# Attention scores from fp32 q and k, loaded once per pair of heads, with 64-row products and two units a round

## The chip, the cores and the metric

The kernel runs on one core of a Trainium2 chip. The metric is device time in microseconds; three executions of the kernel before took 2005.05 us in the median (2004.14 to 2009.55). The engines have a queue each and work through it in order: TensorE (PE, with its weight loads, PEld), VectorE (DVE), ScalarE (ACT), GpSimd (POOL) and SyncE (SP), which here only issues DMA transfers.

## The reference

One layer of a hybrid decoder, for a prompt group (1 sequence of 1024 tokens) and a sample group (8 sequences, one new token each, with 2048 cached keys and values). Only the attention half of the mixer is touched:

```
h = modulate(x, sh1, sc1);  q, k, v, z, xbc, dt_raw = split(h @ w_in)
q = rope(q) * 64**-0.5;  k = rope(k)                       # 16 heads of 64
parts = [dilated attention(q, k, v) for (window, dilation) in ((128, 1), (512, 4), (2048, 16))]
attn = parts merged by weights proportional to their softmax denominators
mix = concat(rms_norm(attn) * g_attn, gated SSD output) @ w_out;  x = x + g1 * mix;  then an MLP and a final norm
```

A prompt query reads itself and the keys at distances d, 2d, ..., window. A sample query reads the same distances in its cache.

## The kernel before, in words

The order of the work is written out by hand: each engine's instructions stand in the order in which the program emits them. A main stream is a generator whose yields state a cost, and `Side` streams are emitted beside it in proportion to these costs. Three stages matter here.

*The q and k projection* (`proj_qk`, 570 to 763 us of the trace). Each of 8 weight blocks goes through four ranges of 256 tokens and two feature halves f; a half is 8 k-tiles of three float32r products (`mm3`, L62 to L64), 48 products for both halves (509 products ran from 600 to 660 us of the trace). DVE multiplies each half with cos and sin (L679), `rotated` mixes them (L627, L628) into the tile `ab`, ACT casts that to a float32r high half `hl` (L634), DVE subtracts for the low half (L635), and the store to `q_d` or `k_d` (L637) follows. What is put off goes into the list `self.later`, one entry of which is emitted at each half of a feature half; its third entry, `turn`, transposes the rotated k on TensorE (L648, L652) for the cache output. Beside the projection run the end of the SSD and `sample_ssd` (ACT L1015, POOL L1016, L1026 and L1027, DVE L1023), then the attention's first loads (`prep(0)`, the mask, `load_v(0)`).

*The attention of the prompt* (`attention`, 763 to 1026 us). A head pair j has 16 units (j, kind, i): eight of kind B (dilations 4 and 16, among the tokens of one residue mod 4) and then eight of kind A (dilation 1). A unit covers 128 queries of both heads and 128 or 256 keys. Keys lie in DRAM residue by residue. `prep` loads per head three float32r tiles of 128 rows: q high over q low, k high over low, and k low over high, 24 transfers for a pair. `scores(n)` makes, for each of the two heads, two products over 128 rows (L1276, L1277); for kind B the stationary q is a slice with a step of four columns. DVE adds the mask, takes the negated maximum and writes P (L1279). `exps(n - 1)` (L1288) follows one unit later, `transposes(n - 3)` (L1297, copied out of PSUM by ACT or DVE, L1299) and `pv(n - 6)` (L1314), the product with v on a 64-column tile for each head. One round of the loop is one unit, and on TensorE it is: scores, transposes, pv. `merge(j)` joins kinds A and B: the statistics of B go through DRAM to reach token order (`st_d`, loaded back into `J`, L1333), some ten small operations on DVE follow (L1338 to L1350), and four groups of four transposes (L1361).

*The sample's scores* (`decode_scores`), a side stream from the 12th unit on. For 24 pieces of the cached keys POOL multiplies 128x1024 values with q (L1089) and halves them twice by additions (L1093), DVE sums the rest (L1095), and the next piece is fetched by a DMA (L1071). Three buffers `dkv` hold the pieces; piece n is summed while piece n + 1 is worked on.

PSUM has eight banks: three for `s`, three for `pt`, two for `o`.

## Time and profile before

| | |
|---|---|
| time of three executions | 2005.05 us median, 2004.14 to 2009.55 |
| profiled execution, span from first to last instruction | 2009.0 us; the page shows no time of it beside the span; the slowest of the three, 2009.55, is the nearest |
| q and k projection | about 570 to 763 us |
| attention of the prompt, with the sample's scores | 763 to 1026 us |
| mean granted TensorE clock over the span | 0.983 of full speed |

The two stages are 456 us of the span; the input projection, the SSD, the output projection and the MLP, which are not changed, make up the rest. The page gives the busy time of each engine; a view by stretch gives it for a part of the span, with the clock that TensorE was granted (1.00 is 2.4 GHz, half of it 1.2 GHz) and the share of the 16 DMA engines. A busy TensorE is not TensorE at its peak: how fast it gets on is read from the distance between the starts of its instructions. An idle time stands with what ended it; "issue" is time in which the engine waited for nothing that the profile shows.

### The profile page before, as it was taken

The numbers are of one execution on the slowest core, as the hardware profiler recorded it, in microseconds if no ns is written. First come the engines' busy times: TensorE is split into PE (matmuls) and PEld (weight loads), VectorE is DVE, ScalarE is ACT, GpSimd is POOL, SyncE is SP. The second block draws the span as 40 slices with busy tenths as digits, with TensorE's granted clock in tenths as the row PEclk, the third lists the DMA queues.
The fourth block names the chain that finished last, engine by engine and source line by source line (L and its number), as shares of the span: only waits on it lengthen the run. The fifth ranks groups of instructions, "written<-read, shape, count | busy, mean of one in ns | idle before, by whom it ended". The sixth has DMA issues, their size and how long they took to land.

```text
span 2009.0 us, 34179 instructions
## 1 busy us (share of the span) xinstructions
PE 1918.1 (95%) x13390; PEld 1792.7 (89%) x13390; DVE 1219.6 (61%) x2966; ACT 700.8 (35%) x1681; POOL 356.8 (18%) x310
## 2 busy tenths in 40 slices
PE   5999999999999789999998999999999999999998
PEld 3689999999999787777786899999999999999997
DVE  4614675674787876767773444655555555555566
ACT  3511425344443335656652232422211122222212
POOL 0010143342320640565610012000000000000000
PEclk8999999999999888999999999999999999999999
DMA  9672222222346869999846310557765566657664
GB/s 285 251 273 82 74 66 64 86 60 77 118 144 192 256 187 222 228 211 228 203 164 219 121 43 22 210 210 251 252 230 210 210 251 250 232 210 251 250 242 169
DMA packets 200267, 366.81 MB, mean 183 GB/s; under 512 B 29728, under 2 KB 163488, under 8 KB 195713
## 3 DMA queue, kind: packets, MB, share of 16 engines
q1 hardware_dynamic: 196524, 351.27, 55.1%
q0 software_dynamic: 3376, 13.30, 2.1%
q8 instruction: 106, 1.74, 0.4%
q14 instruction: 53, 0.43, 0.1%
q10 hardware_dynamic: 208, 0.07, 0.0%
HBM read 321.64 MB, written 177.23 MB: 248 GB/s over the span
## 4 chain that ended last, share of the span: by engine, by line
PE 49%; DMA 5%; DVE 4%; POOL 1%; SPq 1%; issue 1%; ACT 1%; DVEq 0%; POOLq 0%; ACTq 0%
PE acc L62 15%; PE acc L63 14%; PE acc L64 14%; DMA dkv<-in_cache_k_win 2%; PE o L1314 1%; PE pt L1297 1%; PE s L1276 1%; DMA st_d<-st 1%; SPq L1236 1%; PE misc L1162 1%; PE s L1277 1%; PE otr L1534 1%; POOL dkv L1089 1%; DMA dkv<-in_cache_v_win 1%; POOL dkv L1093 0%
## 5 line engine op out<-in xcount | busy, mean ns | idle before, releaser
L1406 DVE SCALAR_TENSOR_TENSOR x<-acc,mod,x 128x352 f32<-128x352 f32 (+2 forms) x432 | 238.8, 561 | 149.0 <-PE acc L64 142.4
L62 PE MATMUL acc<-u,mw_hi 128*128 128x352 f32 (+3 forms) x800 | 251.7, 315 | 0.3 <-DVE gs L1410 0.3
L63 PE MATMUL acc<-u,mw_hi 128*128 128x352 f32 (+3 forms) x800 | 251.1, 314 | 0.0
L64 PE MATMUL acc<-u,mw_lo 128*128 128x352 f32 (+3 forms) x800 | 250.4, 313 | 0.0
L63 PE MATMUL acc<-h_lo,mw_hi 128*128 128x352 f32 (+1 forms) x720 | 230.3, 320 | 0.0
L62 PE MATMUL acc<-h_hi,mw_hi 128*128 128x352 f32 (+1 forms) x720 | 229.8, 319 | 0.0
L64 PE MATMUL acc<-h_hi,mw_lo 128*128 128x352 f32 (+1 forms) x720 | 229.6, 319 | 0.0
L62 PE MATMUL acc<-h_hi,cw_hi 128*128 128x352 f32 (+1 forms) x576 | 191.8, 333 | 1.1 <-ACT cw_hi L442 1.1
L63 PE MATMUL acc<-h_lo,cw_hi 128*128 128x352 f32 (+1 forms) x576 | 184.1, 320 | 0.0
L64 PE MATMUL acc<-h_hi,cw_lo 128*128 128x352 f32 (+1 forms) x576 | 183.7, 319 | 0.2 <-DVE cw_lo L443 0.2
L1723 ACT ACTIVATE ur<-acc 128x352 f32<-128x352 f32 (+1 forms) x96 | 43.8, 456 | 394.3 <-PE acc L64 394.3
L1724 DVE TENSOR_TENSOR ur<-ur 128x352 f32<-128x352 f32 (+1 forms) x96 | 49.6, 516 | 169.0 <-ACT ur L1723 169.0
L62 PE MATMUL acc<-h_hi,qw_hi 128*128 128x256 f32 (+1 forms) x512 | 152.1, 297 | 0.0
L62 PEld LDWEIGHTS acc<-u,mw_hi 128*128 128x128 f32 x800 | 150.4, 188 | 1.1 <-PE acc L64 0.5
L64 PEld LDWEIGHTS acc<-u,mw_lo 128*128 128x128 f32 x800 | 150.6, 188 | 0.0
L63 PEld LDWEIGHTS acc<-u,mw_hi 128*128 128x128 f32 x800 | 150.3, 188 | 0.0
L64 PE MATMUL acc<-h_hi,qw_lo 128*128 128x256 f32 (+1 forms) x512 | 147.0, 287 | 2.0 <-DVE qw_lo L443 2.0
L63 PE MATMUL acc<-h_lo,qw_hi 128*128 128x256 f32 (+1 forms) x512 | 147.1, 287 | 0.0
L1288 ACT ACTIVATE P<-P,st 128x256 f32<-128x256 f32 (+1 forms) x256 | 119.3, 468 | 74.1 <-DVE st L1279 73.9
L63 PEld LDWEIGHTS acc<-h_lo,mw_hi 128*128 128x128 f32 x720 | 135.4, 188 | 0.0
L62 PEld LDWEIGHTS acc<-h_hi,mw_hi 128*128 128x128 f32 x720 | 135.3, 188 | 0.0
L64 PEld LDWEIGHTS acc<-h_hi,mw_lo 128*128 128x128 f32 x720 | 135.2, 188 | 0.0
(422 smaller groups left out, 4604.6 us busy)
## 6 DMA issues: line engine op xcount, KB each, us to landing
aw<-in_w_ada SPq DMA_DIRECT2D x16, 1024.0 KB
mw_raw<-in_w_down SPq DMA_DIRECT2D x16, 1024.0 KB
out_k_win_sample<-in_cache_k_win SPq DMA_DIRECT2D x8, 2044.0 KB
out_v_win_sample<-in_cache_v_win SPq DMA_DIRECT2D x8, 2044.0 KB
mw_raw<-in_w_up SPq DMA_DIRECT2D x15, 1024.0 KB
cw_raw<-in_w_in SPq DMA_DIRECT2D x24, 512.0 KB
dkv<-in_cache_k_win SPq DMA_DIRECT2D x24, 512.0 KB
dkv<-in_cache_v_win SPq DMA_DIRECT2D x24, 512.0 KB
```

Source lines behind the costliest of these rows:

```text
L62: mm(ps, lhi, rhi, start=first, stop=False)
L63: mm(ps, lhi, rlo, start=False, stop=False)
L64: mm(ps, llo, rhi, start=False, stop=last)
L1089: nc.gpsimd.tensor_tensor(pd, pd, qbs[b], op=OP.mult)
L1162: nc.tensor.matmul(p[32 * q:32 * q + 32, 0:256], pp[:, c, q], vt[:, 256 * q:256 * q + 256], start=(c == 0), stop=(c == 2))
L1236: nc.sync.dma_start(f32(t[32 * i:32 * i + 32]), d[j // 2, (i // 2) ^ o, i % 2, h:h + 32])
L1276: nc.tensor.matmul(out, q, cols(ks, kind, lo, hi), start=True, stop=False)
L1277: nc.tensor.matmul(out, q, cols(kw, kind, lo, hi), start=False, stop=True)
L1288: nc.scalar.activation(Ps[n][:, a, :W], Ps[n][:, a, :W], AF.Exp, bias=st[:, i, a, 0:1], scale=-1.0, accum_out=st[:, i, a, 1:2])
L1406: nc.vector.scalar_tensor_tensor(self.x1[:, m, a:e], ps[:, :e - a], self.mod[:, blk, m, 0:1], self.x1[:, m, a:e], op0=OP.mult, op1=OP.add)
L1723: nc.scalar.activation(r[:, :W], ps[:, :W], AF.Relu)
L1724: nc.vector.tensor_tensor(r[:, :W], r[:, :W], r[:, :W], op=OP.mult)
```

## The change

1. `proj_qk` stores the rotated fp32 values themselves, in token order. The cast on ACT, the subtraction on DVE and the tile `hl` are gone, `q_d` and `k_d` are half as large, the store is the first entry of `self.later`, and the first `ab` tile has three buffers.
2. `prep` loads q and k once per pair of heads, fp32, 64 rows for each head, with 8 transfers. POOL copies both into residue order (`qr`, `kr`), for kind B; kind A reads `qs` and `ks` themselves. `load_v` loads kind A's v in token order with one transfer.
3. `scores` takes one fp32 product over 64 rows for each head and unit, the heads in rows 0 to 63 and 64 to 127 and in different PSUM banks; both operands are contiguous.
4. A round is two units. Scores of both come first, then transposes of one unit and pv of another, twice. `exps` follows one round later, transposes two, pv three. `s` has two buffers of two banks, `pt` two.
5. `decode_scores` has six buffers, fetches three pieces ahead and sums a piece two pieces later.
6. `merge` loads `J` three rounds after the store and starts its arithmetic two rounds after the last scores of kind A; it reads A's statistics in place.

```diff
     def proj_qk(self, acc, ws, st):
...
-            hl = st.tile([128, 2, 2, 256], F32R, name="hl", tag="hl", bufs=2)
-            src, view = r[:, :, 0:256], lambda t: t
-            if not isq:
-                src = src.rearrange("p f (u r) -> p f r u", r=4)
-                view = lambda t: t.rearrange("p f (r u) -> p f r u", r=4)
-            nc.scalar.copy(view(hl[:, 0]), src)
-            lo = lambda: self.lo_eng.tensor_tensor(view(hl[:, 1]), src, f32(view(hl[:, 0])), op=OP.subtract)
-            dst = (self.q_d if isq else self.k_d)[c, :, :, :, a:a + 256].rearrange("x f p t -> p (x f) t")
-            store = lambda: nc.sync.dma_start(dst, f32(hl).rearrange("p x f t -> p (x f) t"))
+            dst = (self.q_d if isq else self.k_d)[c, :, :, a:a + 256].rearrange("f p t -> p f t")
+            store = lambda: nc.sync.dma_start(dst, r[:, :, 0:256])
...
-            self.later += [lambda: None, lo, turn, lambda: (store(), out())]
+            self.later += [store, lambda: None, turn, out]
...
-                    t = st.tile([128, 2, 264], F32, name="ab", tag=f"ab{f}", bufs=2 - f)
+                    t = st.tile([128, 2, 264], F32, name="ab", tag=f"ab{f}", bufs=3 - 2 * f)
...
     def decode_scores(self, sb, sc, unit):
-        kv = lambda: sb.tile([128, D], F32, name="dkv", tag="dkv", bufs=3)
+        kv = lambda: sb.tile([128, D], F32, name="dkv", tag="dkv", bufs=6)
...
-        last = None
-        for n in range(25):
+        last = []
+        for n in range(26):
...
-            if last is not None:
-                nc.vector.tensor_reduce(*last, op=OP.add, axis=mybir.AxisListType.X)
-                fetch(n + 1)
-            last = sc[:, c, 16 * b:16 * b + 16], p3[:, :, :16]
+                last.append((sc[:, c, 16 * b:16 * b + 16], p3[:, :, :16]))
+            if n >= 2:
+                nc.vector.tensor_reduce(*last.pop(0), op=OP.add, axis=mybir.AxisListType.X)
+            fetch(n + 3)
...
         def load_v(j):
-            for r in range(4):
-                nc.sync.dma_start(v[32 * r:32 * r + 32], s.rearrange("(t u r) c -> r u t c", u=32, r=4)[r])
+            nc.sync.dma_start(v, s.rearrange("(t p) c -> p t c", p=128))
...
         def prep(j):
-                for n, d, o in (("q", self.q_d, 0), ("k", self.k_d, 0), ("w", self.k_d, 1)):
-                    t = stks[j % 2].tile([128, S], F32R, name=n + "s", tag=n + "s", bufs=2)
-                    for i in range(4):
-                        nc.sync.dma_start(f32(t[32 * i:32 * i + 32]), d[j // 2, (i // 2) ^ o, i % 2, h:h + 32])
...
+            ts = [stk.tile([128, S], F32, name=n + "s", tag=n + "s", bufs=2) for n in ("q", "k")]
+            for t, d in zip(ts, (self.q_d, self.k_d)):
+                for a in range(2):
+                    h = 32 * (2 * (j % 2) + a)
+                    for f in range(2):
+                        p = 64 * a + 32 * f
+                        nc.sync.dma_start(t[p:p + 32], d[j // 2, f, h:h + 32])
+                yield
+            yield
+            rs = [stk.tile([128, S], F32, name=n + "r", tag=n + "r", bufs=2) for n in ("q", "k")]
+            for t, r in zip(ts, rs):
+                nc.gpsimd.tensor_copy(r.rearrange("p (r u) -> p r u", r=4), t.rearrange("p (u r) -> p r u", r=4))
+                yield
+            heads[j] = ts, rs
...
-                nc.tensor.matmul(out, q, cols(ks, kind, lo, hi), start=True, stop=False)
-                nc.tensor.matmul(out, q, cols(kw, kind, lo, hi), start=False, stop=True)
...
+            s = ps_s.tile([128, 2, 2, 256], F32, name="s", tag="s")
+            P = Ps[m] = pb.tile([128, 2, 2, 256], F32, name="P", tag="P", bufs=LT + 1)
+            q, k = heads[j][kind]
+            ws = []
+            for u in range(2):
+                lo, hi = span(units[2 * m + u])
+                ws.append(128 * (hi - lo))
+                for a in range(2):
+                    h = slice(64 * a, 64 * a + 64)
+                    nc.tensor.matmul(s[:, a, u, :ws[u]], cols(q, i + u, i + u + 1)[h], cols(k, lo, hi)[h], start=True, stop=True)
...
         def merge(j):
-            for _ in range(4):
+            for _ in range(3):
...
+            while (j, A) not in done:
                 yield
+            for _ in range(2):
+                yield
+            st = stats.pop((j, A)), J
...
+            nc.vector.tensor_tensor(m, st[A][:, :, :, 0], st[B][:, :, :, 0], op=OP.min)
+            for k in (A, B):
+                nc.vector.tensor_tensor(e[:, k], m, st[k][:, :, :, 0], op=OP.subtract)
...
+            for k in (A, B):
+                nc.vector.tensor_tensor(l[:, k], st[k][:, :, :, 1], e[:, k], op=OP.mult)
+            nc.vector.tensor_tensor(m, l[:, A], l[:, B], op=OP.add)
...
-        for n in range(N + LP):
+        for m in range(M + LP):
...
+            for u in range(2):
+                if 0 <= m - LT < M:
+                    transposes(m - LT, u)
+                if 0 <= m - LP < M:
+                    pv(m - LP, u)
...
-            yield 1400
+            yield 2800
...
-        ps_s = self.pool(es, "a_ps", bufs=3, space=PSUM)
+        ps_s = self.pool(es, "a_ps", bufs=2, space=PSUM)
...
-                ps_t = self.pool(ef, "a_pt", bufs=3, space=PSUM)
+                ps_t = self.pool(ef, "a_pt", bufs=2, space=PSUM)
```

Comments and docstrings are gone too, which moves the line numbers.

On TensorE, in a pair's part B before (s are the scores, pt the transposes of P, or of oT in a merge, o the product with v; a row of fp32 scores or of o stands for one product or several):

```order
L1276 MATMUL s_8566<-ks_8031,qs_8016 128x128
L1277 MATMUL s_8566<-ws_8051,qs_8016 128x128
L1276 MATMUL s_8566<-ks_8093,qs_8073 128x128
L1277 MATMUL s_8566<-ws_8118,qs_8073 128x128
L1297 MATMUL pt_8576<-ident_72,P_8471 128x128 x4
L1314 MATMUL o_8522<-PT_8483,vB_8167 64x128 x2
L1361 MATMUL pt_8585<-ident_72,oT_8189 128x128 x4
L1276 MATMUL s_8599<-ks_8031,qs_8016 128x256
L1277 MATMUL s_8599<-ws_8051,qs_8016 128x256
L1276 MATMUL s_8599<-ks_8093,qs_8073 128x256
L1277 MATMUL s_8599<-ws_8118,qs_8073 128x256
L1297 MATMUL pt_8609<-ident_72,P_8506 128x128 x2
```

The same place now (`qr` and `kr` are the copies in residue order); two products of 128 and two of 256 columns make a round:

```order
L1265 MATMUL s_8963<-kr_8684,qr_8683 128x128 x2
L1265 MATMUL s_8963<-kr_8684,qr_8683 128x256 x2
L1287 MATMUL pt_8977<-ident_72,P_8873 128x128 x2
L1303 MATMUL o_8938<-PT_8936,vA_8324 64x128 x4
L1287 MATMUL pt_8986<-ident_72,P_8873 128x128 x4
L1303 MATMUL o_8938<-PT_8948,vA_8324 64x128 x4
L1265 MATMUL s_9006<-kr_8684,qr_8683 128x128 x2
```

Four score products a unit have become two, and one block of them stands for two units; transposes and o then take turns twice before the next scores, where they took one turn before.

On DVE, in the projection before (L679, L627 and L628 are the rotation, xS and mS belong to `sample_ssd`):

```order
L679 TENSOR_TENSOR ab_6512<-acc_6457,rope_t_5091 128x2x256
L627 TENSOR_TENSOR ab_6447<-ab_6447,ab_6512 128x256
L628 TENSOR_TENSOR ab_6447<-ab_6447,ab_6512 128x256
L961 TENSOR_TENSOR xS_6275<-preS_77,vec_75 128x128
L963 TENSOR_TENSOR mS_6518<-sc_6481,vec_75 128x128
L964 TENSOR_TENSOR xS_6275<-xS_6275,mS_6518 128x128
L635 TENSOR_TENSOR hl_6516<-ab_6447,hl_6516 128x512
L963 TENSOR_TENSOR mS_6518<-sc_6481,vec_75 128x128
L964 TENSOR_TENSOR xS_6275<-xS_6275,mS_6518 128x128
L679 TENSOR_TENSOR ab_6550<-acc_6522,rope_t_5091 128x528
```

The same place now (the first row is the rotation's product, line 672 now):

```order
L672 TENSOR_TENSOR ab_6470<-acc_6416,rope_t_5091 128x2x256
L627 TENSOR_TENSOR ab_6406<-ab_6406,ab_6470 128x256
L628 TENSOR_TENSOR ab_6406<-ab_6406,ab_6470 128x256
L954 TENSOR_TENSOR xS_6240<-preS_77,vec_75 128x128
L956 TENSOR_TENSOR mS_6475<-sc_6439,vec_75 128x128
L957 TENSOR_TENSOR xS_6240<-xS_6240,mS_6475 128x128
L956 TENSOR_TENSOR mS_6475<-sc_6439,vec_75 128x128
L957 TENSOR_TENSOR xS_6240<-xS_6240,mS_6475 128x128
L672 TENSOR_TENSOR ab_6506<-acc_6479,rope_t_5091 128x528
```

The subtraction that stood three to four operations behind L628 is gone, and the operations of `sample_ssd` follow the rotation at once.

On POOL, a piece of the sample's scores before (L1365 adds the two parts of a merge):

```order
L1089 TENSOR_TENSOR dkv_8870<-dkv_8870,dqb_8502 128x1024
L1365 TENSOR_TENSOR o_tok_7980<-o_tok_7980,mt_8922 128x4x128
L1093 TENSOR_TENSOR dkv_8870<-dkv_8870 128x16x32
L1093 TENSOR_TENSOR dkv_8870<-dkv_8870 128x16x16
L1365 TENSOR_TENSOR o_tok_7980<-o_tok_7980,mt_8986 128x4x128
L1089 TENSOR_TENSOR dkv_8996<-dkv_8996,dqb_8502 128x1024
L1093 TENSOR_TENSOR dkv_8996<-dkv_8996 128x16x32
```

The same engine now, beside the loads of a next pair (L1235 are the copies into residue order):

```order
L1082 TENSOR_TENSOR dkv_8417<-dkv_8417,dqb_8269 128x1024
L1235 COPY qr_8683<-qs_8540 128x1024
L1086 TENSOR_TENSOR dkv_8417<-dkv_8417 128x16x32
L1086 TENSOR_TENSOR dkv_8417<-dkv_8417 128x16x16
L1354 TENSOR_TENSOR o_tok_7865<-o_tok_7865,mt_8676 128x4x128
L1235 COPY kr_8684<-ks_8541 128x1024
L1082 TENSOR_TENSOR dkv_8499<-dkv_8499,dqb_8269 128x1024
L1086 TENSOR_TENSOR dkv_8499<-dkv_8499 128x16x32
L1086 TENSOR_TENSOR dkv_8499<-dkv_8499 128x16x16
L1354 TENSOR_TENSOR o_tok_7865<-o_tok_7865,mt_8775 128x4x128
```

Two copies of 128x1024 for each pair stand between the steps of the pieces, behind a multiplication that waits for its piece's transfer.

## Rows read from the trace of the kernel before

**Rows 1.** Busy time of PE, PEld, DVE, ACT, POOL by stretch; granted clock, DMA share, GB/s.

```profile
...
660.00:745.00 85.00, 67.51 (x491) 65.31 (x490) 71.28 (x71) 31.87 (x82) 48.98 (x21) 0.86 0.73 216
...
763.00:771.00 8.00, 4.68 (x18) 3.97 (x16) 3.03 (x15) 2.63 (x5) 0.00 (x0) 0.66 1.11 238
771.00:1026.00 255.00, 240.99 (x1908) 195.57 (x1909) 186.37 (x695) 167.33 (x608) 126.29 (x88) 0.97 0.86 206
...
```

**Rows 2.** Waits, q and k projection: who waited for whom, us, times, longest.

```profile
...
PE acc L652 <- DVE ab L627: 8.7, 2, 6.3
...
PE acc L648 <- DVE ab L628: 4.2, 2, 2.1
...
PE acc L648 <- DVE ab L627: 3.8, 4, 1.5
...
PE acc L652 <- DVE ab L628: 2.1, 1, 2.1
...
```

**Rows 3.** DVE by line, 660 to 745 us: form, count, busy, mean ns, idle before.

```profile
...
L628 DVE TENSOR_TENSOR ab<-ab 128x256 f32<-128x256 f32 (+1 forms) x10 | 14.5, 1452 | 0.0
L635 DVE TENSOR_TENSOR hl<-ab,hl 128x512 fp32r<-128x512 f32 x11 | 14.2, 1289 | 7.4 <-ACT hl L634 7.3
...
```

**Rows 4.** TensorE timeline, part B: start us, us, instruction.

```profile
...
994.88 0.45 PE L1276 MATMUL s<-ks,qs 128*128 128x128 f32 x1
...
995.87 0.62 PE L1297 MATMUL pt<-ident,P 128*128 128x128 f32 x4
...
997.01 0.51 PE L1276 MATMUL s<-ks,qs 128*128 128x256 f32 x1
...
998.07 0.38 PE L1297 MATMUL pt<-ident,P 128*128 128x128 f32 x2
...
```

**Rows 5.** TensorE timeline, part A and a merge.

```profile
...
1009.50 0.65 PE L1361 MATMUL pt<-ident,oT 128*128 128x128 f32 x4
1009.91 0.37 PE L1276 MATMUL s<-ks,qs 128*128 128x256 f32 x1
...
1011.38 0.39 PE L1276 MATMUL s<-ks,qs 128*128 128x256 f32 x1
1011.60 0.29 PE L1277 MATMUL s<-ws,qs 128*128 128x256 f32 x1
...
1011.97 0.60 PE L1297 MATMUL pt<-ident,P 128*128 128x128 f32 x4
1012.50 0.44 PE L1314 MATMUL o<-PT,vB 128*64 128x128 f32 x4
...
```

**Rows 6.** Weight loads on TensorE, part B.

```profile
...
997.22 0.33 PEld L1277 LDWEIGHTS s<-ws,qs 128*128 128x128 f32 x1
...
```

**Rows 7.** Weight loads on TensorE, part A.

```profile
...
1011.49 0.19 PEld L1277 LDWEIGHTS s<-ws,qs 128*128 128x128 f32 x1
...
```

**Rows 8.** TensorE timeline, fp32 products of an SSD chunk.

```profile
...
238.29 0.66 PE L839 MATMUL y_ps<-dec,xdt 128*64 128x128 f32 x8
238.88 0.70 PE L846 MATMUL y_ps<-xw,Bt 128*128 128x256 f32 x2
...
```

**Rows 9.** TensorE by line: form, count, busy, mean ns of one, idle before.

```profile
...
L846 PE MATMUL y_ps<-xw,Bt 128*128 128x256 f32 x64 | 22.4, 431 | 0.0
...
```

**Rows 10.** SyncE's DMA issues before the attention.

```profile
...
762.59 0.42 SPq L1372 DMA_DIRECT2D mask<-in_k_mask  x1
...
```

**Rows 11.** DVE timeline, first scores.

```profile
...
769.02 0.29 DVE L1279 CUSTOM_DVE_ANT_0 P<-s,mask 128x128 f32<-128x128 f32 x1 [4.08 <-DMA mask<-in_k_mask]
...
```

**Rows 12.** Waits in the attention.

```profile
...
DVE dsc L1095 <- POOL dkv L1093: 26.2, 11, 4.9
...
DVE m L1340 <- DMA J<-st_d: 22.9, 7, 5.9
...
```

**Rows 13.** POOL by line, attention.

```profile
...
L1089 POOL TENSOR_TENSOR dkv<-dkv,dqb 128x1024 f32<-128x1024 f32 x24 | 57.2, 2382 | 76.7 <-DMA dkv<-in_cache_k_win 71.0 <-DVE st L1279 5.7
L1093 POOL TENSOR_TENSOR dkv<-dkv 128x512 f32<-128x512 f32 (+1 forms) x48 | 48.7, 1014 | 3.3
...
```

More of the change, by code (lines that the diff above doesn't have):

```diff
@@ new lines, in scores @@
+            P = Ps[m] = pb.tile([128, 2, 2, 256], F32, name="P", tag="P", bufs=LT + 1)
[8 more added lines that the diff above has]
+            for u in range(2):
+                for a in range(2):
+                    W = ws[u]
+                    nc.vector.tensor_tensor_reduce(out=P[:, u, a, :W], in0=s[:, a, u, :W], in1=mask[:, kind, 256 - W:256], scale=-0.125,
+                                                   scalar=3e38, op0=OP.add, op1=OP.min, accum_out=stats[j, kind][:, i + u, a, 0:1])
@@ L1294, in transposes, with exps @@
+        def exps(m):
+            j, kind, i = units[2 * m]
+            st = stats[j, kind]
+            for u in range(2):
+                lo, hi = span(units[2 * m + u])
+                W = 128 * (hi - lo)
+                for a in range(2):
+                    P = Ps[m][:, u, a, :W]
+                    nc.scalar.activation(P, P, AF.Exp, bias=st[:, i + u, a, 0:1], scale=-1.0, accum_out=st[:, i + u, a, 1:2])
+        def transposes(m, u):
+            lo, hi = span(units[2 * m + u])
             p = ps_t.tile([128, 2, 2, 128], F32, name="pt", tag="pt")
```

156 lines of the change are left out of this document (51 added, 105 removed).

## The prediction

> **What bounds the kernel now.** I read the busy time by stretch first, then the waits in each of the two stages that the change touches, then TensorE's timeline in the attention, and last the lines of DVE and POOL. By stretch [rows 1] the reader is to see that TensorE is the engine that sets the pace in both stages: it is busy 67.5 of 85 us in the middle of the projection and 241.0 of 255 us in the attention, while DVE has 186.4 and POOL 126.3 of these 255. So two things can be won: time in which TensorE stands still or runs at its lower clock, and work of TensorE itself.
>
> In the projection, from 660 to 745 us, it stands still for 17.5 us, and the granted clock is 0.86 [rows 1]. The waits name the reason: the transposes of the rotated k wait for DVE's L627 and L628, 8.7 + 4.2 + 3.8 + 2.1 = 18.8 us over the stage [rows 2]. DVE is late there: 71.3 us busy of 85 [rows 1], and another 7.4 us stood still at L635, which waits for ACT's cast [rows 3].
>
> In the attention TensorE's own work is the bound, and its timeline shows where it goes. From the first score product of a unit to its first transpose take 0.99 and 1.06 us in part B [rows 4], but 0.59 us in part A [rows 5], although the products are of the same number and of the same size or smaller. The weight loads differ: 0.33 us where q is a slice with a step of four [rows 6], 0.19 us where it is contiguous [rows 7]. In part A the first product stands 0.22 us ahead of the second and the other three steps are 0.12 us each ((0.59 - 0.22) / 3).
>
> **The change, part by part.**
>
> *(a) Projection, cast and subtraction gone: -15 us.* From 660 to 745 us, 11 subtractions cost DVE 14.2 us, and its wait at them 7.4 us [rows 3], 21.6 together. DVE's 71.3 + 7.4 = 78.7 us fall to 57. TensorE's own need for the same products is below the 67.5 us in which it was busy, so that DVE now has room where it had none. What can be won at most: 0.14 x 85 = 11.9 us of clock were not granted, which is 23.8 us at half rate; at most 17.5 of these were idle, so at least 6.3 us of work ran at 1.2 GHz, which costs 3.1. With 18.8 us of waits the ceiling is 22 us. Not all of it will go: POOL works 49 us of the 85 beside DVE [rows 1], and DVE operations with two inputs in SBUF are slow there (L628 takes 1452 ns for 256 elements, L635 1289 for 512 [rows 3], so it is not the elements that cost). I take two thirds, bounds -22 and 0. The stores to q_d and k_d are emitted two steps earlier, right behind the rotation; SyncE waits there for L628 instead of for L635, and behind it stand the next weights, which are loaded two tiles ahead. I cost that at nothing; if this cover is too thin it shows as waits for qw_raw.
>
> *(b) Start of the attention: -3 us.* The mask is issued at 762.59 us [rows 10], behind 24 loads of q and k, and DVE's first score operation waits for it until 769.02 us [rows 11]. In these 8 us TensorE is busy 4.7 us at clock 0.66 [rows 1]: 3.3 us idle, and 0.34 x 8 = 2.7 us of clock lost, or 5.4 us at half rate, of which 2.1 us were work, so 1.0 more. Ceiling 4.4 us. Sixteen loads fewer bring the mask forward, but two copies on POOL now stand between the loads and the first scores. Bounds -4.4 and +1.
>
> *(c) Scores: -16 us.* Before, a pair of units costs 0.99 + 1.06 = 2.05 us in part B and 1.18 us in part A. After, two units are four fp32 products. An fp32 product is two instructions (L846 shows x2 for one product [rows 8]), so there are eight. The trace has no two row tiles side by side. The nearest rows: column tiles of 64, where eight instructions of 128 columns and the following change of tile take 238.88 - 238.29 = 0.59 us, 0.074 each at most [rows 8]; and the full array, where the two of 256 columns take 0.70 us whole and 0.43 us one [rows 8, 9], so the second starts 0.27 us after the first. I take 0.12 us, the step of part A, which a contiguous weight load of 128 columns allows. Eight are 0.96 us, and 0.10 us more for the first one. The array then changes from 64 rows to the full array: four transposes are 0.41 us up to scores of the same tile (1009.50 to 1009.91) and 0.53 us up to o (1012.50 - 1011.97) [rows 5], so a change costs 0.12; I take 0.2, since a longer product has to run out. The second transposes now follow an o, and begin with another 0.10. That makes 1.36 us a round. Part B wins 0.69 us in each of 4 rounds, part A loses 0.18 in 4, 2.04 us for a pair, 16 us for eight pairs. Bounds: 0.074 us each and changes at 0.1 give 0.89 us a round, (1.16 + 0.29) x 4 x 8 = -46 us; 0.27 us for 256 and 0.135 us for 128 columns give 2.02 and 2.56 us, +43 us.
>
> *(d) Waits in the attention: -7 us.* TensorE is idle 255 - 241 = 14 us there, and clock 0.97 loses 7.7 us, 15.3 us at half rate, so at least 1.3 us of work, 0.6 more. DVE stood 26.2 us at the sum L1095 for POOL and 22.9 us at L1340 for the statistics' way through DRAM [rows 12], in front of the score operations of the next units. Both are now taken later, the sum two pieces behind and the statistics three rounds after their load. What is late next: POOL gets 16 copies of 128x1024. Against it stand L1089 at 2382 ns for two inputs of that size and L1093 at 1014 ns for half or a quarter [rows 13]; I take up to 2.4 us each, 38 us, so POOL goes from 126 to 164 us of about 230. Each pair's copies stand behind a multiplication that waits for its piece, but are emitted four rounds before their first use. I take half of the 14.6 us; bounds -15 and +10.
>
> The Trainium skill (GPSIMD Engine Reference, section 4.1) calls operations with one input on GpSimd roughly line-rate, and section 3.1 gives 1.03 cycles an element; the estimate by it is 0.9 us for 1024 elements, 14 us for all 16 copies. The sum stays as it is by that, with POOL further from the bound.
>
> *(e) End of the attention: +2 us.* The last pair's arithmetic begins two rounds after its last scores instead of before them. Bounds 0 and 6, the longest of the waits for J [rows 12].
>
> Softmax, transposes, the copies out of PSUM and pv keep their number and sizes. The transfers fall from 24 to 8 of 128 KB for a pair, which I cost at nothing beside (b) and (d).
>
> Sum: -15 - 3 - 16 - 7 + 2 = -39 us, from 2009.0 to 1970. The median of the runs is 4 us under this span, so 1966.
>
> **The rivals.**
>
> *Another engine takes over.* If the round is bound by POOL's and DVE's order rather than by TensorE, (c) and (d) bring nothing and the attention keeps its 255 us: -15 - 3 + 2 = -16, 1989. For it: DVE at 186 us would be busy four fifths of a stage of 232 us, POOL at 164 us over two thirds, and `pt` has one buffer less. Against it: 49 us of DVE's idle time go with two waits [rows 12], so it has the room.
>
> *The row tiles overlap in part.* At 0.16 us instead of 0.12, 64 rounds of eight cost 20 us more: 1986. For it: no row shows two row tiles. Against it: the column tiles' 0.074 us [rows 8]. The Trainium skill (TensorE: Matmul & The Clock Gate, Measured speedup vs the span model) reports 3.07 times for four row tiles, which is 0.77 of full; the estimate by it is 0.12 / 0.77 = 0.16 us. No run here shows it.
>
> *The row tiles do not overlap, and the kernel gets slower.* Place: the eight score instructions of each round; price 0.27 us for 256 columns, the full array's step [rows 8, 9], so (c) is +43: -39 + 59 = +20, 2025. It decides from 0.12 + 39 / 512 = 0.20 us an instruction. Against it: products on column tiles pass each other; for it: nothing but that the case is unseen.
>
> *The projection's waits stay*, because POOL and not L635 makes DVE late: (a) is 0, 1981.
>
> **How the numbers follow.** The forecast as worked out has 0.56; another engine 0.18; partial overlap 0.10; waits that stay 0.07; no overlap 0.09. About 0.3%, 6 us, is what a measurement of this kernel tells from no change, so faster ends at 1999. All cases but the last lie below it with nearly all their chance, so faster has 0.85; the upper tails of the first two rivals give 0.06 for no change; no overlap and its neighbours 0.09 for slower. The forecast's own range is 1945 to 1987 from the bounds of (a), (c) and (d) taken in part; with the first three rivals the range is 1942 to 1999, which leaves out no overlap and the far ends.
>
> **What would show it.** (a) L648 and L652 no longer wait for L627 and L628, and the clock from 660 to 745 us is near 1.00. (c) Eight score instructions step by about 0.12 us, a round of part B takes 0.7 us less and one of part A about 0.2 us more than two units before. (d) The waits for dsc and J are gone from DVE. The prediction is wrong if score instructions step by 0.2 us or more, if TensorE waits for P or PT in each round, or if scores of part B wait for POOL's copies.

## The result, and the profile after

The changed kernel takes 1991.34 us (median of four runs, 1986.38 to 1993.01) where the kernel before takes 2006.28 (2004.14 to 2009.55): 0.9927 of it, 95% interval 0.9908 to 0.9945. It is faster by 15 us; 39 were forecast. The profiled execution of the change has a span of 1984.6 us and is the fastest of its four, while the one before, with 2009.0, lies near its slowest, so the two traces differ by 24.4 us, 9 more than the medians.

| stage | before | after | difference | forecast |
|---|---|---|---|---|
| first score product of TensorE | 763.0 | 751.6 | -11.4 | |
| first score operation of DVE (end of terms a and b) | 769.02 | 752.57 | -16.4 | -18 |
| from there to the first product of the output projection (c, d, e) | 259.2 us | 256.0 us | -3.2 | -21 |
| the rest of the kernel | 980.8 us | 976.0 us | -4.8 | 0 |

The loss stands in the third row. Kernels with one and the same projection put their first score product between 750.0 and 755.0 us (twelve traces, below), and the rest of the kernel takes 974.4 to 979.5 us in the experiments, so a few us of a single trace's stage are scatter. By stretch, with the columns of [rows 1], after the change:

```profile
...
660.00:745.00 85.00, 74.64 (x580) 72.55 (x579) 69.50 (x81) 23.00 (x67) 49.34 (x22) 0.94 0.69 202
751.60:1008.60 257.00, 225.29 (x1938) 148.01 (x1937) 203.59 (x720) 165.42 (x613) 155.81 (x103) 0.93 0.55 147
...
```

In the projection TensorE is busy 74.6 us of 85 at a granted clock of 0.94, before 67.5 at 0.86 [rows 1]. In the attention it now stands idle for 31.4 us (the sum over its waits from 751.6 to 1008.6; 17.3 before, from 763.0 to 1028.2), and the granted clock is 0.93 instead of 0.96. So its own work shrank, but it stood longer. Its timeline shows the shrinking. First two rounds of part B, then one of part A with the four transposes of a merge (L1349) ahead of it:

```profile
...
874.61 0.93 PE L1265 MATMUL s<-kr,qr 64*128 64x128 f32 x8
875.46 0.66 PE L1287 MATMUL pt<-ident,P 128*128 128x128 f32 x4
876.05 0.66 PE L1303 MATMUL o<-PT,vA 128*64 128x128 f32 x8
...
877.81 0.93 PE L1265 MATMUL s<-kr,qr 64*128 64x128 f32 x8
878.67 0.44 PE L1287 MATMUL pt<-ident,P 128*128 128x128 f32 x2
...
898.62 0.65 PE L1349 MATMUL pt<-ident,oT 128*128 128x128 f32 x4
899.21 1.13 PE L1265 MATMUL s<-ks,qs 64*128 64x256 f32 x8
900.27 0.66 PE L1287 MATMUL pt<-ident,P 128*128 128x128 f32 x4
...
```

The eight score instructions of a round take 0.86 us in part B and 1.06 in part A up to the first transpose, where two units took 0.99 + 1.06 [rows 4] and 2 x 0.59 [rows 5].

The longer standing is in the waits of the attention up to 1005 us (who waited for whom, us, times, longest):

```profile
...
ACT e L1335 <- DVE e L1334: 37.6, 7, 6.7
...
PE pt L1349 <- ACT PT L1289: 26.1, 8, 4.9
...
```

Once for each pair of heads but the last, TensorE waits ahead of the merge's transposes for a copy that ACT makes (an eighth wait is 0.2 us), and ACT before that for `e`, which DVE makes. DVE's waits for dsc and J [rows 12] are gone, as forecast. Here is one such place on four engines. TensorE:

```profile
...
882.98 0.66 PE L1303 MATMUL o<-PT,vB 128*64 128x128 f32 x8
886.67 1.11 PE L1349 MATMUL pt<-ident,oT 128*128 128x128 f32 x4 [3.03 <-ACT PT L1289]
887.72 1.65 PE L1265 MATMUL s<-ks,qs 64*128 64x128 f32 x8
889.30 0.69 PE L1287 MATMUL pt<-ident,P 128*128 128x128 f32 x2
...
```

ACT:

```profile
...
879.20 0.37 ACT L1289 COPY PT<-pt 128x256 f32<-128x256 f32 x1
884.38 0.23 ACT L1335 ACTIVATE e<-e 128x32 f32<-128x32 f32 x1 [4.81 <-DVE e L1334]
884.52 0.39 ACT L1280 ACTIVATE P<-P,st 128x128 f32<-128x128 f32 x1
...
886.27 0.35 ACT L1289 COPY PT<-pt 128x256 f32<-128x256 f32 x1
...
```

DVE:

```profile
...
880.93 0.68 DVE L48 COPY oT<-o 128x512 f32<-128x512 f32 x1
881.53 0.77 DVE L1332 TENSOR_TENSOR m<-st,J 128x16 f32<-128x16 f32 x1
882.33 1.93 DVE L1334 TENSOR_TENSOR e<-m,st 128x16 f32<-128x16 f32 x1
884.18 0.16 DVE L1334 TENSOR_TENSOR e<-m,J 128x16 f32<-128x16 f32 x1
...
```

POOL:

```profile
...
879.90 2.37 POOL L1082 TENSOR_TENSOR dkv<-dkv,dqb 128x1024 f32<-128x1024 f32 x1
882.20 2.02 POOL L1235 COPY qr<-qs 128x1024 f32<-128x1024 f32 x1
884.19 2.08 POOL L1086 TENSOR_TENSOR dkv<-dkv 128x512 f32<-128x512 f32 x2
...
```

Read from the bottom: DVE's `m` has 16 elements in each of 128 rows and takes 0.77 us; it ends at 882.30, where POOL's L1082 ends (879.90 + 2.37 = 882.27). The next one, of the same size, takes 1.93 and ends at 884.26, where POOL's copy ends (884.22). The third, issued just there, takes 0.16. ACT has nothing else to do in this order until 884.38, and the exponentials and the PT copy of the round stand behind it. TensorE stands 3 us and goes on at half speed: four transposes take 1.05 us instead of 0.59 (898.62 to 899.21 above) and eight score instructions 1.58 instead of 0.86. The granted clock of the 10 us around it (882 to 892) is 0.83, between stretches at 1.00. This happens six times: around the end of each of the six waits of 3.0 to 4.9 us begins a stretch of 3.4 or 6.8 us with a granted clock of 0.50 (1.2 GHz).

### The profile page after: what moved, and what is told of

Same layout as the page of the kernel before. It is cut to its first block, busy times and chain, and to the rows that moved or that the text cites. A ratio compares the mean times of both kernels' runs of the same rounds, so it can differ in the third digit from the quotient of the medians.

```text
span 1984.6 us, 33763 instructions
## 1 busy us (share of the span) xinstructions
PE 1892.2 (95%) x13390; PEld 1738.4 (88%) x13390; DVE 1209.6 (61%) x2942; ACT 670.0 (34%) x1649; POOL 388.2 (20%) x326
## 4 chain that ended last, share of the span: by engine, by line
PE 84%; DVE 7%; ACT 3%; DMA 3%; issue 2%; POOL 1%; SPq 0%; DVEq 0%; POOLq 0%; ACTq 0%
PE acc L62 23%; PE acc L64 22%; PE acc L63 22%; PE pt L1287 3%; PE o L1303 3%; PE s L1265 3%; PE pt L1349 1%; ACT P L1280 1%; PE y_ps L839 1%; DVE ab L628 1%; DMA aw<-in_w_ada 1%; PE y_ps L832 1%; DMA vw_raw<-in_w_in 1%; PE ada_acc L146 1%; PE misc L1155 1%
```

## The experiments

All times are medians; ratios are to runs of the kernel before on the same chip, with their 95% interval. "Idle" is TensorE's idle time from its first score product to its first product of the output projection, from the trace. The letters of theories and rivals are those of the expectations, which stand ahead of each measurement.

| | edit | us | ratio | first score | attention | idle |
|---|---|---|---|---|---|---|
| | the change | 1991.3 | 0.9927 | 751.6 | 257.0 | 31.4 |
| e1 | exponential of the merge a round later | 1976.6 | 0.9860 [0.9845, 0.9876] | 755.0 | 244.6 | 23.8 |
| e2 | POOL's work for the sample's scores left out | 1957.5 | 0.9770 [0.9749, 0.9792] | 750.4 | 222.7 | 9.9 |
| e3 | e1, both transposes first | 1969.7 | 0.9825 [0.9810, 0.9841] | 754.4 | 236.8 | 28.5 |
| e4 | cast and subtraction back | 2004.1 | 0.9990 [0.9978, 1.0003] | 765.3 | 259.5 | 33.7 |
| e5 | e1, small operations on POOL, two more rounds | 1953.3 | 0.9741 [0.9719, 0.9763] | 750.0 | 220.5 | 7.7 |
| e6 | e1, sums one piece behind | 1973.4 | 0.9840 [0.9819, 0.9861] | 751.3 | 243.4 | 22.1 |
| e7 | e1 without POOL's copies | 1976.0 | 0.9853 [0.9832, 0.9875] | 752.4 | 245.3 | 6.3 |
| e8 | e5, both transposes first | 1955.7 | 0.9752 [0.9733, 0.9770] | 753.5 | 223.5 | 20.8 |
| e9 | POOL's state recurrence left out | 1975.7 | 0.9855 [0.9830, 0.9881] | 739.5 | 259.7 | 34.0 |
| e10 | e1 with e5's rounds, on DVE | 1986.0 | 0.9909 [0.9879, 0.9939] | 753.4 | 255.2 | 28.6 |
| e11 | e8, one round more | 1952.6 | 0.9739 [0.9713, 0.9766] | 751.6 | 218.5 | 18.6 |
| e12 | the kernel before, small operations on POOL | 2008.6 | 1.0017 [1.0002, 1.0032] | 763.9 | 265.2 | 15.9 |
| e13 | recurrence in quarters | 1985.5 | 0.9890 [0.9867, 0.9912] | 745.5 | 259.4 | 33.9 |
| e14 | POOL's score work in pieces | 2017.1 | 1.0054 [1.0037, 1.0070] | 753.5 | 283.7 | 53.9 |
| e15 | e5 and e13 | 1947.5 | 0.9707 [0.9680, 0.9734] | 743.0 | 220.6 | 7.8 |
| e16 | small operations on POOL, the change's rounds | 1948.2 | 0.9707 [0.9685, 0.9728] | 750.2 | 218.5 | 5.4 |
| e17 | e16 and e13 | 1944.1 | 0.9702 [0.9686, 0.9719] | 743.0 | 218.5 | 5.4 |
| e18 | e17, both transposes first | 1941.0 | 0.9689 [0.9674, 0.9704] | 746.9 | 218.9 | 18.1 |

### Is it ACT's wait, or POOL? e1, e2

```
                 nc.vector.tensor_tensor(e[:, k], m, st[k][:, :, :, 0], op=OP.subtract)
+            yield
             nc.scalar.activation(e, e, AF.Exp)
```

> Edit: ACT's exponential of the merge (L1335 of the changed kernel) is emitted one round after DVE's two differences e (L1334) instead of in the same round. Theory A (the merge's exponential holds up ACT): the seven or eight waits of ACT for e, 37.6 us, go; TensorE's idle time ahead of L1349, 28.3 us in all, falls below 8, and the half-clock stretch behind each of these waits goes (about 8 us); about 28 us come off: 1991 becomes 1960 to 1970. Rival B (DVE or POOL bounds the rounds, the wait is only where it shows): TensorE's idle time turns up ahead of other lines, total idle in the attention stays near 30 us, 1985 to 1993.

Measured: 1976.6. Half of what theory A gave. The waits ahead of L1349 are gone (2.2 us are left of 28.3), but the idle time is still 23.8: 20.9 us of it now stand ahead of L1287, most of it (15.3 us in 7 waits) for DVE's PT copy, which stands behind the same `m`, `e`, `e` and now also behind `l` (1.25 to 1.59 us in six merges, where the change has 0.16 to 0.18 in all but one). So part of rival B held: the wait moved from ACT to DVE.

```
-                nc.gpsimd.tensor_tensor(pd, pd, qbs[b], op=OP.mult)
-                for w in (32, 16):
-                    nc.gpsimd.tensor_tensor(p3[:, :, :w], p3[:, :, :w], p3[:, :, w:2 * w], op=OP.add)
```

> Leaves out POOL's multiplications and additions for the sample's scores (L1082, L1086; 106 us of POOL work), so the sample's output is not the attention's; the loads and DVE's sums stay. Theory A with POOL as its amplifier (DVE's two-input operations of 16 elements wait until POOL's running instruction ends): m and e (L1332, L1334) take 0.16 to 0.2 us instead of 0.86, 1.49 and 0.73, ACT's wait for e falls from 5 to about 2.5 us a pair, TensorE's idle ahead of L1349 from 28 to about 8 to 12 us: 1968 to 1978. Without POOL's part in it (the small DVE operations are slow by themselves): m and e keep their durations and the time stays within 5 us of 1991.

Measured: 1957.5, 10 us better than the expectation's best. DVE by line and form in the change (count, busy, mean ns of one, idle before):

```profile
...
L1334 DVE TENSOR_TENSOR e<-m,st 128x16 f32<-128x16 f32 x8 | 11.9, 1486 | 0.3
...
L1332 DVE TENSOR_TENSOR m<-st,J 128x16 f32<-128x16 f32 x8 | 6.9, 856 | 0.0
L1334 DVE TENSOR_TENSOR e<-m,J 128x16 f32<-128x16 f32 x8 | 5.8, 725 | 0.0
...
```

and in e2:

```profile
...
L1329 DVE TENSOR_TENSOR m<-st,J 128x16 f32<-128x16 f32 x8 | 1.8, 230 | 0.0
...
L1331 DVE TENSOR_TENSOR e<-m,st 128x16 f32<-128x16 f32 x8 | 1.4, 175 | 0.3
...
L1331 DVE TENSOR_TENSOR e<-m,J 128x16 f32<-128x16 f32 x8 | 1.3, 168 | 0.0
...
```

The same operations take 0.57 us together instead of 3.07. They are not slow by themselves: they wait for POOL. In the change's trace every `m` and `e` that takes over 0.3 us ends within 0.05 us of the end of a POOL instruction.

### Engine or rounds? e5, e10, e16

```
-            nc.vector.tensor_tensor(m, st[A][:, :, :, 0], st[B][:, :, :, 0], op=OP.min)
-            for k in (A, B):
-                nc.vector.tensor_tensor(e[:, k], m, st[k][:, :, :, 0], op=OP.subtract)
+            nc.gpsimd.tensor_tensor(m, st[A][:, :, :, 0], st[B][:, :, :, 0], op=OP.subtract)
+            nc.gpsimd.tensor_scalar(e[:, A], m, 0.0, -1.0, op0=OP.max, op1=OP.mult)
+            nc.gpsimd.tensor_scalar(e[:, B], m, 0.0, 1.0, op0=OP.min, op1=OP.mult)
...
-                nc.vector.tensor_tensor(l[:, k], st[k][:, :, :, 1], e[:, k], op=OP.mult)
+                nc.gpsimd.tensor_tensor(l[:, k], st[k][:, :, :, 1], e[:, k], op=OP.mult)
```

(the sum of `l` and the last factor likewise; the reciprocal stays on DVE). e5 has e1's `yield` and two more, ahead of the reciprocal and of the transposes; e10 has the same three and leaves the operations on DVE; e16 moves the operations and has none of the three.

> e1, and the merge's small operations with two inputs (difference of the statistics, e, l, their sum, the last factor) run on POOL instead of DVE, each step a round later; e is made as exp of min and max of the difference, the same value. Theory A2 (what is left after e1 is DVE standing in m, e, e and l until POOL's instruction of about 2.4 us ends, with the PT copy behind it that TensorE waits for): DVE has no operation of 16 elements longer than 0.3 us, TensorE's waits ahead of L1287 for DVE's PT, 2.2 to 3.6 us once a pair, go; idle in the attention from 23.8 to 8 to 12 us and some 4 us of half clock less: 1956 to 1964 against e1's 1976.6. Rival B2 (POOL's queue is late, so that the merge's factor comes late there): TensorE waits ahead of L1350, 1972 to 1980.

> e1 with the same two more rounds between the merge's steps as e5, but with its small operations left on DVE. Theory A2 (e5's 23 us came from the other engine, since DVE stands behind POOL's instructions wherever the small operations are put): m and e keep 0.6 to 1.5 us each, 1972 to 1978. Rival M (they came from the two rounds of room): 1953 to 1960.

> The changed kernel with the merge's small operations on POOL, but all steps in the rounds in which the change has them (exponential right behind e, transposes right behind the last factor). With e1, e5 and e10 it fills a table of engine and rounds. If both are needed (ACT waits in order for whichever engine makes e): ACT waits for POOL's e 2 to 5 us a pair, 1968 to 1990. If the engine alone is the cause: 1953 to 1960.

| | the change's rounds | exponential later | three rounds more |
|---|---|---|---|
| on DVE | 1991.3 | 1976.6 (e1) | 1986.0 (e10) |
| on POOL | 1948.2 (e16) | | 1953.3 (e5) |

The engine decides. 43 us come off where the operations change engine in the change's own rounds, 38 with the rounds; rounds alone give 5 to 15. (The formula of `e` changes with the engine: one difference and two operations with one input, where DVE has a minimum and two differences. That form was not run on DVE.) e10 is 9 us slower than e1, outside its expectation: with the more rounds the last factor (128x32, 0.19 us in the change) stands behind POOL too, 0.8 to 2.1 us in five merges. One branch of e16's expectation had it wait on ACT at 1968 us or more; its ACT does wait for POOL's `e`, but 11.0 us in all instead of 37.6, TensorE's waits ahead of the merge are almost gone, and the time is 5 us below the other branch:

```profile
...
PE pt L1349 <- ACT PT L1289: 2.1, 3, 1.1
PE pt L1349 <- DVE o_tok L1350: 1.0, 1, 1.0
...
```

On POOL each such operation takes 0.21 to 0.28 us (medians), and the clock of the whole attention is 1.00:

```profile
...
750.20:968.70 218.50, 212.13 (x1937) 140.53 (x1936) 175.64 (x665) 165.34 (x613) 169.78 (x159) 1.00 0.66 171
...
```

### What sets the wait behind POOL? e13, e14

Both issue POOL's long operations in pieces, with the same arithmetic.

```
-                nc.gpsimd.tensor_tensor(s4, s4, t2, op=OP.add)
+                for g in range(4):
+                    nc.gpsimd.tensor_tensor(s4[:, g], s4[:, g], t2[:, g], op=OP.add)
```

> The changed kernel with each of POOL's three operations of the state recurrence (L1009, L1019, L1020, 128x1024, 1.9 to 2.6 us) issued as four of 128x256; the same arithmetic. Theory P (a DVE operation with two inputs in SBUF waits until the instruction that POOL is at has ended, so that its length sets the wait): L627 and L628 stand at most about 1.1 us instead of 2.6, TensorE's waits for ab before the first score fall from 11.7 to 3 to 7 us, 1981 to 1988. Rival Q (POOL's load sets it, DVE gets through only when POOL has nothing to do): waits as before or longer, since four short operations take POOL longer than one, 1990 to 1998.

```
-                nc.gpsimd.tensor_tensor(pd, pd, qbs[b], op=OP.mult)
+                for i in range(0, D, 256):
+                    nc.gpsimd.tensor_tensor(pd[:, i:i + 256], pd[:, i:i + 256], qbs[b][:, i:i + 256], op=OP.mult)
```

> The changed kernel with POOL's multiplication of the sample's scores in four pieces of 128x256 and its two additions in four and two pieces. Theory P: no DVE operation of 16 elements takes over 0.9 us, m and e of a merge take 1.0 to 1.8 us together instead of 3.1, ACT's wait for e falls by about 1.5 us a pair, 1975 to 1986. Rival Q: they take as long or longer, 1988 to 2000.

They disagree. In e13 theory P holds for the lengths: beside the recurrence L628 takes at most 0.96 us instead of 2.62. DVE in e13 (640 to 740 us):

```profile
...
L628 DVE TENSOR_TENSOR ab<-ab 128x256 f32<-128x256 f32 (+1 forms) x15 | 13.4, 894 | 0.0
...
```

The first score product comes 6.1 us earlier, and 4.5 earlier than in any trace with the change's projection (1985.5; its interval and the change's overlap slightly). TensorE's waits for ab fall only from 11.7 to 9.5 us, less than expected, but the clock granted from 660 to 745 us is 0.98 instead of 0.94. In e14 theory P fails badly: 2017.1, and `m` alone takes 4.75 us on average of seven. DVE in e14:

```profile
...
888.24 0.68 DVE L48 COPY oT<-o 128x512 f32<-128x512 f32 x1
888.84 7.84 DVE L1335 TENSOR_TENSOR m<-st,J 128x16 f32<-128x16 f32 x1
896.71 0.17 DVE L1337 TENSOR_TENSOR e<-m,st 128x16 f32<-128x16 f32 x1
...
954.99 13.73 DVE L52 TENSOR_TENSOR y_lo<-yt,y_hi 128x704 fp32r<-128x704 f32 x1
...
```

and POOL in e14:

```profile
...
886.97 2.57 POOL L1089 TENSOR_TENSOR dkv<-dkv 128x128 f32<-128x128 f32 x6
889.44 2.83 POOL L1083 TENSOR_TENSOR dkv<-dkv,dqb 128x256 f32<-128x256 f32 x4
892.16 2.02 POOL L1238 COPY qr<-qs 128x1024 f32<-128x1024 f32 x1
894.10 2.55 POOL L1089 TENSOR_TENSOR dkv<-dkv 128x128 f32<-128x128 f32 x6
...
```

POOL works without a gap from 886.97 to 896.65, and `m`, begun at 888.84, ends at 896.68: it was not let in at the ends of the twelve instructions between. Three more merges have the same wait (7.81 to 7.83 us), and `y_lo`, of another stage, stands 13.73 us over 24 instructions; TensorE's longest wait of e14, 11.1 us, lies behind that one. All five end where POOL has run out of work: its next instruction starts 6 to 10 us later. Shorter waits of the same run (`e` with 0.65 and 0.76 us at 784) end while POOL goes on at once. So such a wait ends at the end of a POOL instruction, but not always of the one under way: rival Q holds for the long ones, theory P for the others. What decides stays open.

### The projection: e4, e9

e4 puts `nc.scalar.copy(view(hl[:, 0]), src)` and the subtraction into `hl[:, 1]` back.

> The changed kernel with ACT's cast and DVE's subtraction put back into the projection (their result is read by nothing, one buffer, no extra stores). Theory E (these two were what made DVE late in the projection): the first score product comes 8 to 14 us later than at 751.6 us, TensorE's waits for ab go from 11.7 back to about 18.8 us, 1999 to 2005. Rival F (DVE is late in the projection because of POOL's work beside it, and the saving came from fewer stores): within 4 us of 1991.

Measured: 2004.1, first score product at 765.3; 12.8 us come back, as theory E has it. The waits in the projection (TensorE, e4) are those of [rows 2] again:

```profile
...
PE acc L652 <- DVE ab L627: 8.8, 2, 6.3
PE acc L648 <- DVE ab L628: 5.9, 3, 2.1
...
```

e9 takes out `t2S` and POOL's three operations on it (L1009, L1019, L1020).

> The changed kernel without POOL's three operations of the sample's state recurrence (L1009, L1019, L1020; 56 us of POOL work beside the projection from about 650 to 735 us), so the sample's output and its states are not the reference's; loads, ACT's scaling and DVE's sums stay. Theory K (what stayed of the projection's waits is DVE's rotation, L627 and L628 with two inputs, standing behind POOL's 2 to 2.6 us operations): L628's longest falls from 2.6 us to under 0.8, TensorE's waits for ab from 11.7 to under 3 us, the first score product comes 9 to 16 us earlier than 751.6, time 1975 to 1983. Rival L (DVE is late there from its own work): waits stay above 8 us, within 4 us of 1991.

Measured: 1975.7, first score product at 739.5, 12.1 us earlier. The rotation on DVE (650 to 745 us) takes in the change

```profile
...
L628 DVE TENSOR_TENSOR ab<-ab 128x256 f32<-128x256 f32 (+1 forms) x12 | 20.2, 1684 | 0.0
L627 DVE TENSOR_TENSOR ab<-ab 128x256 f32<-128x256 f32 (+1 forms) x13 | 17.9, 1380 | 0.4
...
```

and in e9 (640 to 735 us)

```profile
...
L628 DVE TENSOR_TENSOR ab<-ab 128x256 f32<-128x256 f32 (+1 forms) x15 | 8.1, 540 | 0.0
L627 DVE TENSOR_TENSOR ab<-ab 128x256 f32<-128x256 f32 (+1 forms) x15 | 8.1, 539 | 0.5
...
```

Theory K holds: what stayed of term (a)'s waits is POOL again. TensorE's waits for ab fall from 11.7 to 3.2 us (under 3 were expected).

### The parts of the attention: e6, e7

e6 takes the sums and loads of `decode_scores` back to one piece behind and two ahead.

> e1, and DVE's sums of the sample's scores are taken one piece behind POOL and loaded two pieces ahead, as in the kernel before. Theory G (taking the sums later was worth its part of the waits): DVE waits for POOL at L1089 for 15 to 30 us in all, TensorE's idle time rises by 5 to 15 us, 1982 to 1990. Rival H (the delay brought nothing, since a piece is ready when the next is multiplied): DVE's wait at L1089 under 5 us, within 3 us of 1976.6.

Measured: 1973.4, with an interval that overlaps e1's; DVE does not wait for POOL at the sum. Rival H: this part of the change brought nothing here.

```
+            if kind == B:
+                t = t.rearrange("p (u r) -> p r u", r=4)[:, lo // 2]
+                lo, hi = lo % 2, lo % 2 + hi - lo
             return t[:, 128 * lo:128 * hi]
```

> e1 without POOL's copies of q and k: part B's products read q and k in place with a step of four columns. Theory I (part B's gain comes from contiguous weight loads, 0.19 instead of 0.33 us): eight score instructions of a round of part B take 2.0 to 2.6 us instead of 0.86, +36 us or more less some 8 us for POOL's 34 us of copies: 2000 to 2030. Rival J (it comes from the halves of the array, whose loads overlap): 0.86 to 1.2 us for eight, 1965 to 1985.

Measured: 1976.0, the time of e1, by effects that cancel. TensorE in e7, a round of part B:

```profile
...
872.04 1.75 PE L1263 MATMUL s<-ks,qs 64*128 64x128 f32 x8
873.72 0.44 PE L1285 MATMUL pt<-ident,P 128*128 128x128 f32 x2
...
```

The eight instructions take 1.68 us instead of 0.86, 0.82 x 32 rounds = 26 us. Against that, idle falls from 23.8 to 6.3 us, and with the clock at 1.00 instead of 0.96 some 8 us that e1's steps lose at half clock are gone. POOL has 34 us of copies less, and the merge's small operations with two inputs on DVE take 21 us in all instead of 39; but TensorE's longer rounds also give the other engines more time, and the two are not told apart. Theory I was nearer on where part B's gain comes from, but 10 us too high in price. It is not shown to be the weight loads alone: e7 reads q and k with a step, where the kernel before did so for q only, and a weight load takes 0.25 us in e7 and 0.19 in e1 (medians).

### The order of the transposes, and the best version: e3, e8, e11, e12, e15, e17, e18

```
             for u in range(2):
                 if 0 <= m - LT < M:
                     transposes(m - LT, u)
+            for u in range(2):
                 if 0 <= m - LP < M:
                     pv(m - LP, u)
```

> e1, and in each round both transposes are emitted before both products with v (s, pt, pt, o, o instead of s, pt, o, pt, o). Theory C (each change between transposes on the full array and column tiles of 64 costs TensorE 0.1 to 0.2 us, as four transposes take 0.59 us up to an o but 0.41 up to the next product on the full array): two changes fewer in each of 64 rounds, 10 to 20 us less than e1: 1945 to 1960 if e1 gives 1965. Rival D (the two transposes of a round need two free PSUM buffers at once, so that TensorE waits for the copies of the round before): waits ahead of L1287 of 0.3 us or more in most rounds, the time within 5 us of e1 or above it.

> e5 with the order of e3 (both transposes of a round, then both products with v). If the two are independent: e5 less 10 us, 1946 to 1954. If DVE or POOL bounds the round by now: within 3 us of e5.

> e8 (two transposes, then two products; merge's small operations on POOL) with one more round between the merge's factor and its first transposes. Theory N (e8 lost its 10 us at DVE's o_tok, which waits for POOL's last factor about 1 us a pair and holds up the PT copy behind it): the waits ahead of L1287 for o_tok fall from 8.3 to under 3 us, 1944 to 1950. Rival O (they come from the two PSUM buffers that merge and rounds share): 1953 to 1958.

> e17 with both transposes of a round ahead of both products with v. If e8's and e11's lost gain came from the extra rounds of e5: 10 us less than e17, 1930 to 1936. If it came from two PSUM buffers that merge and rounds share: within 4 us of e17.

In e3 TensorE's steps without waits fall from 220.6 us (e1) to 208.1 and its waits rise by 4.7; 6.9 us come off e1 in the medians. Theory C is right on the steps; part of what they gain goes in waits. On top of e5 the order brings nothing (e8, idle 20.8 instead of 7.7); one round more does not bring it back (e11 against e5: overlapping intervals, idle 18.6), nor does the lack of the extra rounds (e18 against e17: overlapping, idle 18.1). That fits the PSUM buffers that merge and rounds share, but it is not shown: no run had a third buffer, as `s` takes four of the eight banks and `pt` and `o` two each.

e12 does to the kernel before what e5 does to e1.

> The kernel before with only the merge's small operations of two inputs moved to POOL (as in e5), nothing else of the change. If the kernel before lost time at the same place (DVE's 22.9 us of waits for J and small operations of 0.3 to 0.7 us): DVE does not wait for J, TensorE's idle time in the attention falls from 17.3 to 6 to 10 us, 1990 to 1998. If its merge, spread over more steps, cost TensorE nothing: within 4 us of 2006.

Measured: 2008.6, no gain; ACT there waits for POOL:

```profile
...
ACT e L1346 <- POOL e L1344: 32.7, 7, 8.8
...
```

with POOL's own waits for its pieces (65.1 us) ahead of it. So what helped the change by 38 to 43 us brought nothing there. That the merge on DVE cost nothing in the kernel before is not shown by this, as POOL's waits took its place. e15 and e17 join the two remedies.

> e5 and e13 together: small operations of the merge on POOL, the recurrence in quarters. If P holds and the two stages are independent: e5's 1953 less e13's gain, 1943 to 1951. If Q holds: 1952 to 1960.

> e16 and e13 together: the merge's small operations on POOL in the change's own rounds, the state recurrence in quarters. If the two causes lie in different stages and add: 1948.2 less e13's 5.9, 1939 to 1945. If they share what they win (a clock or a transfer behind both): 1946 to 1950.

1947.5 and 1944.1, 6 us under e5 and 4 under e16. As ratios, which compare runs on one chip, these gains lie within overlapping intervals; in the traces the first score product comes 7.0 and 7.2 us earlier, as in e13. e17 and e18 are the best here, 3% under the kernel before; their intervals overlap.

## Why the prediction was wrong

The direction, the range and the sizes of (a), (b) and (e) held; the sum did not: 15 us instead of 39. The step that failed is (d), which had the wrong sign. That 1991 lies in the stated range is luck: (c) gained some 14 us more than forecast, which hid about half of the 30 us that (d) was off.

- **(a) and (b), projection and start: -18 forecast, -16.4 in the traces,** 11.4 of it up to TensorE's first product. Putting the cast and the subtraction back costs 12.8 us of the median (e4). The reason given, DVE late in front of the transposes, is shown. What I set down as "slow beside POOL" and left at a third is worth 12 us more (e9). The clock from 660 to 745 us rose to 0.94, not to 1.00, and 11.7 of the 18.8 us of waits for ab stayed.
- **(c) scores: -16 forecast; TensorE's steps shrank by 35, about 30 of it at equal clock.** Without its waits TensorE's steps in the attention are 247.4 us before and 212.1 in e16, which has the change's products with hardly a wait: scores 102.7 to 60.0, transposes 62.7 to 66.8, the merge's 14.0 to 18.7, pv 67.9 to 66.6. About 5 us of the 35 are the clock: e16 ran at 1.00, and in these stretches of the kernel before (columns of [rows 1]) the steps took about 5 us longer than the same steps elsewhere in its trace (an estimate, step by step against their mean there):

```profile
...
765.50:775.70 10.20, 8.11 (x33) 7.45 (x33) 4.38 (x25) 6.29 (x24) 0.00 (x0) 0.50 1.13 297
902.00:905.40 3.40, 3.40 (x19) 2.74 (x17) 3.30 (x7) 1.19 (x7) 3.24 (x3) 0.50 0.93 236
987.40:994.20 6.80, 6.80 (x36) 5.28 (x35) 5.24 (x21) 4.77 (x18) 3.88 (x3) 0.50 0.99 167
...
```

  The score step was 0.107 to 0.133 us an instruction against 0.12 taken; the 0.3 us a round that I added for a tile change and a second fill cost 0.06 at each of the transposes instead (0.59 us, 0.53 before [rows 5]). Part A, where I saw a loss of 0.18 us a round, lost nothing: 1.06 against 2 x 0.59, which the transposes take back. Of the gain, 26 us go with contiguous operands (e7); the rest was not taken apart.
- **(d) waits: -7 forecast; TensorE's idle time grew by 14 us, and its work at half clock costs about 8 us more.** Its steps without waits are 225.3 us in the change and 212.1 in e16, so 13 us are lost behind the waits, where the kernel before lost about 5. With -30 for (c) these give the 8 us by which the attention got shorter, counted from TensorE's first product (265.2 to 257.0). The waits for dsc and J went, but I asked only what POOL's load would do to POOL. I did not ask what stands behind the merge's three small operations, which the change emits in one round with the exponential: ACT in order behind DVE, DVE behind POOL. L628 with 1452 ns for 256 elements [rows 3] showed the mechanism, and I priced it in (a) and not in (d). The Trainium skill (SBUF — State Buffer, "SBUF: two separate sides") states it: a DVE operation with two inputs in SBUF and a GpSimd operation that reads SBUF exclude each other, for a whole instruction. It was the rule against this change, and I weighed another. The trace agrees at each long `m` and `e` of the change, and e14's 7.84 us goes beyond it. Of (d)'s prices, the work at half clock was too low, 0.6 us, taken from the least that could have run there. The price of the copies held: 2.0 to 2.2 us each against up to 2.4 taken, and over twice the 0.9 us of the estimate that stands beside it.
- **(e) end of the attention: +2 forecast, +2.1 measured** (from the end of the last o to the output projection 2.66 us before, 4.75 after).
- **The rivals.** "Another engine takes over" gave 1989 and comes nearest to 1991, by chance: it kept the attention at 255 us because DVE and POOL would have too much to do, but (c) was won in full and lost again in waits, and e16 runs at 1948 with POOL busier (169.8 us of 218.5, against 155.8 of 257.0). Row tiles that overlap in part (0.16 us, also the estimate by the Trainium skill, TensorE: Matmul & The Clock Gate, "Measured speedup vs the span model") or not at all (0.27) are excluded by the 0.107 to 0.133 us.
- **Not forecast:** 4.8 us after the attention. A wait for the sample's values fell from 5.3 to 3.1 us; the rest is not traced, and part of it is scatter (the stage takes 974.4 to 979.5 us in the experiments, 976.0 here, 980.8 before).

## What to carry to other kernels

Ahead of moving work to POOL, list DVE's operations with two inputs in SBUF near it: each can stand there for as long as POOL's instructions last (0.8 to 1.9 us in the change, 7.8 in e14), however few elements it has, and what waits for it in order on ACT or TensorE stands too. Tiny operations that stood so were better off on the engine that caused the wait (43 us, e16), but not where that engine itself stood waiting for transfers (e12, no gain). Where a step of several engines is gathered into one round, read for each engine what is queued behind its wait.

## What the runs showed that was not expected

- A 128x16 operation with two inputs in SBUF took 0.16 us alone on DVE and up to 7.84 us beside an unbroken row of POOL instructions; shorter POOL instructions made it worse in one place (e14, +26 us) and better in another (e13, -6 us).
- Eight score instructions over 64 rows took 1.68 us with operands in steps of four columns and 0.86 with contiguous ones.
- The version with 34 us of POOL copies (e1) has 26 us less of TensorE's score steps than the one without (e7), and 17.5 us more of waits and 8 us more of steps at the lower clock: the attention takes 245 us in both.
